# Three gemm groups of a decoder layer turned round, and the first modulation vector summed in two halves, with late constants loaded from another queue

## The chip, the cores and the metric

The program runs on one core of one Trainium2 chip. The metric is the device time of one execution in microseconds, the median of several runs. One further execution was recorded by the hardware profiler; its own time is 1817.8 us and its span, from the first to the last instruction, is 1816.1 us.

## What is computed

One layer of a decoder on 256 tokens of width 2048 in float32, cut here to what the change touches (S = 256, D = 2048):

```python
mod = silu(c) @ w_ada + b_ada                        # six vectors of 2048: sh1, sc1, gt1, sh2, sc2, gt2
h = rmsnorm(x, g_mix) * (1 + sc1) + sh1
z = h @ w_in                                         # mq mk mv mo mi mf dq dk dv sq sk sv gm gd gs
mqk = silu(causal_dwconv(concat(mq, mk), w_mconv))   # width 4, along the tokens
out_m, out_d, out_s = mlstm(...), differential_attention(...), stick_breaking_attention(...)
merged = (sigmoid(gm) * (out_m @ w_branch[0])
          + sigmoid(gd) * (out_d @ w_branch[1])
          + sigmoid(gs) * (out_s @ w_branch[2]))
x = x + gt1 * (merged @ w_out)
h = rmsnorm(x, g_ffn) * (1 + sc2) + sh2
x = x + gt2 * ((silu(causal_dwconv(h @ w_up[:, :DFF])) * (h @ w_up[:, DFF:])) @ w_down)
```

## The kernel before

Every large product keeps float32 accuracy with a rounded type: each operand is split into a high part (type fp32r, written by ScalarE) and a low part (the rest, written by VectorE as source minus high), and a product is three matmuls: high by high, high weight by low activation, low weight by high activation. `weights` (L310) loads a block of up to 512 rows by 512 columns through the SyncE queue into `raw`, and makes `hi` (L324, ScalarE) and `lo` (L326, VectorE) of it, two k-tiles of 128 rows at a time. `gemm` (L332) walks the contraction in steps of four k-tiles and has three forms for a chunk of 512 output columns:

- form F: a 128x128 block of weights is stationary and 256 tokens of one part of the activation move; the output has features on partitions. With 16 k-tiles that is 16 x 4 x 3 = 192 matmuls of 256 columns (L371).
- form T: 128 tokens of the activation are stationary and 512 weight columns move; the output has tokens on partitions. 16 x 2 x 3 = 96 matmuls of 512 columns (L369).
- form H: weights are stationary and both parts of the activation lie side by side, so that a high weight block takes them in one matmul of 512 columns and a low one takes the high part alone (256 columns): 64 + 64 matmuls (L355). Only the second half of the layer (the `w_up` product) uses it. Its output bank holds two halves, which ScalarE (L970) and VectorE (L971) add together.

Order of the work: x is loaded and normalised; `ada_first(0)` multiplies the first 256 columns of `sh1` and `sc1` out of `w_ada`: VectorE multiplies each k-tile of the weight by its scalar of silu(c) and adds it to one accumulator tile, 16 steps one after another (`ada_mac`, L206), and TensorE then sums that accumulator over the partitions with four small matmuls (`ada_sums`, L224; each shows as two instructions in the trace). From that `make_h` (L422) forms k-tiles 0 and 1 of h. Then the first thirteen chunks of `w_in` (sq, sk, sv and the block of gates and d-vectors) are worked through in stages of k-tiles 0 to 1, 2 to 3, 4 to 7, 8 to 11 and the rest (`partial`, L484), while VectorE goes on with the remaining columns of sh1 and sc1. `late_vectors` (L137) loads fourteen small constant vectors on the SyncE queue into a tile of slot 3, which x holds until it is transposed, and puts them on partitions.

Next come, each chunk with its weights: the four gate chunks of gs (`gates`, L797), the branch of stick-breaking attention (`branch`, L803, which multiplies the branch product by its gate), mo and mv in form T, mq and mk in form F with the convolution read straight from PSUM (L868 to L883), the branch of differential attention with its gates, the branch of the mLSTM with its gates, `w_out` in form T, and the feed-forward half. All gates and branch products are in form F. In the last branch (order 2) the finished merged sum, which has features on partitions already, is split into the two parts that `w_out` needs. `w_out` and `w_down` are in form T. Two queues of generators, `side` (the three mixers) and `ada` (the other modulation vectors), are pumped by `tick` at fixed rates between the steps of the gemms, so their VectorE, ScalarE and small TensorE work is traced between the large products; a compile-time scheduler then fixes each engine's order. `tc.issue_after` only fixes order on one engine; it adds no wait.

The two parts of h lie in two tiles `hh` and `hl`, each all sixteen k-tiles of one part.

Of the kernel before, what the change touches and what calls it, by code (L numbers as in the profile page):

```python
# [10 lines left out]
F32 = mybir.dt.float32  # L11
F32R = mybir.dt.float32r
# [5 lines left out]
P = 128  # L18
# [21 lines left out]
def kernel(  # L40
# [97 lines left out]
    def late_vectors():  # L138
        rows = slot(3, "rows2")
        rowsB, rowsC = rows[0:27, 0:P], rows[0:64, P:2 * P]  # L140
        rowsD = rows[0:NF, 2 * P:5 * P].rearrange("k (j p) -> k j p", j=3)
        ld = nc.sync.dma_start
        ld(rowsB[0:16], g_ffn[0].rearrange("(k p) -> k p", p=P))
        ld(rowsB[16:24], g_mout[0].rearrange("h (k p) -> (h k) p", p=P))
        ld(rowsB[24:25], g_dsub)
        for r in range(2):
            ld(rowsB[25:26, r * 64:(r + 1) * 64], g_dq)
            ld(rowsB[26:27, r * 64:(r + 1) * 64], g_dk)
        ld(rowsC, w_mconv[0].rearrange("j (k p) -> (j k) p", p=P))
        ld(rowsD, w_ffconv[0].rearrange("j (k p) -> k j p", p=P))  # L150
        ld(bif, b_gate_if.rearrange("o (g h) -> h (o g)", h=MH))
        lamv = rows[0:1, 640:896].rearrange("o (v d) -> o v d", v=4)
        for i, lv in enumerate((lam_q1, lam_k1, lam_q2, lam_k2)):
            ld(lamv[:, i, :], lv)
        yield
        pv = adaps.tile([P, 512], F32, tag="adaps", name="pv")
        T.transpose(pv[:, 0:27], rowsB, ident[:27, :27])
        T.transpose(pv[:, 27:91], rowsC, ident[:64, :64])
        for j in range(3):
            T.transpose(pv[:, 91 + NF * j:91 + NF * (j + 1)], rowsD[:, j, :], ident[:NF, :NF])  # L160
        A.copy(cols, pv[:, 0:223])
        yield
        V.tensor_scalar(gsub_c, gsub_c, 1.0 - LAM_INIT, None, ALU.mult)
        V.tensor_scalar(gdq_c, gdq_c, 64.0 ** -0.5, None, ALU.mult)

        lp = rows[0:1, 896:1024].rearrange("o (v d) -> o v d", v=2)
        V.tensor_tensor(lp, lamv[:, 0::2, :], lamv[:, 1::2, :], ALU.mult)
        ls = const.tile([1, 2], F32, name="ls")
        V.tensor_reduce(ls, lp, AX.X, ALU.add)
        A.activation(ls, ls, AF.Exp)  # L170
        nl = const.tile([1, 1], F32, name="nl")
        V.scalar_tensor_tensor(nl, ls[:, 1:2], -LAM_INIT, ls[:, 0:1], ALU.add, ALU.subtract)
        yield
        plam = adaps.tile([P, 512], F32, tag="adaps", name="plam")
        T.matmul(plam[:, 0:1], lhsT=ones[0:1, :], rhs=nl, start=True, stop=True)
        V.tensor_copy(nlam, plam[:, 0:1])
# [28 lines left out]
    def ada_mac(accs, raw, kt0, nk):  # L205
        for k in range(nk):  # L206
            kt = kt0 + k
            acc = accs[kt % len(accs)]
            if kt < len(accs):
                V.tensor_scalar(acc, raw[:, k, :], ccol[:, kt:kt + 1], None, ALU.mult)  # L210
            else:
                V.scalar_tensor_tensor(acc, raw[:, k, :], ccol[:, kt:kt + 1], acc, ALU.mult, ALU.add)  # L212

    def partition_sums(acc):

# [20 lines left out]
    def ada_first(k0):  # L236

        accs = [adap.tile([P, 512], F32, tag="acc", name="acc", bufs=2)]
        for q in range(4):
            raw = rawp.tile([P, 4, 512], F32, tag="raw", name="raw")  # L240
            step = 2 if k0 == 0 and q == 3 else 4
            for j in range(0, 4, step):
                for i in range(2):
                    r0, c0 = q * 512 + j * P, i * D + k0 * P
                    with tc.issue_after(state["load"].ins) if k0 else nullcontext():
                        load = nc.sync.dma_start(raw[:, j:j + step, i * 256:(i + 1) * 256],
                                                 w_ada[r0:r0 + step * P, c0:c0 + 256].rearrange("(k p) f -> p k f", p=P))
            if k0 == 0:
                state["load"] = load
            with tc.issue_after(state["first"].ins) if k0 == 2 and q == 0 else nullcontext():  # L250
                ada_mac(accs, raw, 4 * q, 4)
            yield
        ada_sums(accs, k0, 2)
# [131 lines left out]
    def split(hi, lo, src):  # L385

        A.copy(hi, src)
        return V.tensor_tensor(lo, src, hi.bitcast(F32), ALU.subtract)


    hh = slots.tile([P, KD, S], F32R, tag="hh", name="hh")
    hl = slots.tile([P, KD, S], F32R, tag="hl", name="hl")
    hact = (lambda kt: hh[:, kt, :], lambda kt: hl[:, kt, :])
    xnT = [slot(8, "xnT0"), slot(9, "xnT1")]
    xnT_k = lambda kt: xnT[kt // 8][:, (kt % 8) * S:(kt % 8 + 1) * S]

# [25 lines left out]
    def make_h(kt0, kt1):  # L422
        ts = []
        for kt in range(kt0, kt1):
            t = small("ht")
            ts.append(t)
            if kt0 == 0:
                A.activation(hh[:, kt, :], xnT_k(kt), AF.Identity, scale=a1[:, kt:kt + 1], bias=b1[:, kt:kt + 1])
                V.tensor_scalar(t, xnT_k(kt), a1[:, kt:kt + 1], b1[:, kt:kt + 1], ALU.mult, ALU.add)
                state["split"] = V.tensor_tensor(hl[:, kt, :], t, hh[:, kt, :].bitcast(F32), ALU.subtract)  # L430
            else:
                A.activation(t, xnT_k(kt), AF.Identity, scale=a1[:, kt:kt + 1], bias=b1[:, kt:kt + 1])
                state["split"] = split(hh[:, kt, :], hl[:, kt, :], t)
        if kt0 == 0:
            state["first"] = state["split"]
        state["h"] = kt1
# [3 lines left out]
    next(h0)  # L440
    norm_x(xt)
    for _ in h0:
        pass


    sqT, skT, sv = slot(0, "sqT"), slot(1, "skT"), slot(2, "sv")[:, 0:2048]
# [37 lines left out]
    def partial(ci, kt0, kt1):  # L484
        orient, col0, n, dest, scale = first[ci]
        while state["h"] < kt1:
            pump(ada, 1)
        pin = kt0 == 0 and ci == 1
        if kt0 == 0 and ci < 2:
            kept[ci] = [bank("kept"), bank("kept")]  # L490
        acc = gemm(orient, hact, w_in, 0, col0, n, kt0, kt1, hold=state["first"] if pin else None, hold_all=pin,
                   acc=kept.get(ci))
        for b in range(2):
            for cs, d in dest(b):
                if ci in kept:
                    if kt1 == KD:
                        A.activation(d, shaped(acc[b][:, cs], d), AF.Copy, scale=scale)
                elif kt0 == 0:
                    A.activation(d, shaped(acc[b][:, cs], d), AF.Copy, scale=scale)  # L499
                else:  # L500
                    V.scalar_tensor_tensor(d, shaped(acc[b][:, cs], d), scale, d, ALU.mult, ALU.add)  # L501
        tick()
# [288 lines left out]

    mg = []

    def mg_of(ch, b):
        return mg[ch // 2][:, (ch % 2) * 1024 + b * 512:(ch % 2) * 1024 + (b + 1) * 512]

    def gates(col_g, ch, dst):  # L797
        acc = gemm("F", hact, w_in, 0, col_g + ch * 512, 512, 0, KD)
        for b in range(2):
            A.activation(dst(ch, b), acc[b], AF.Sigmoid)  # L800
        tick()

    def branch(bi, col_g, act, order):  # L803
        for ch in range(4):
            if order == 0:
                sg = [mg_of(ch, 0), mg_of(ch, 1)]
            else:
                sg = [wide("sg"), wide("sg")]
                gates(col_g, ch, lambda c_, b: sg[b])
            accb = gemm("F", act, w_branch[bi], 0, ch * 512, 512, 0, KM)  # L810
            for b in range(2):
                d = mg_of(ch, b)
                V.tensor_tensor(sg[b], accb[b], sg[b], ALU.mult)
                if order:
                    V.tensor_tensor(d, d, sg[b], ALU.add)
                if order == 2:
                    h0 = (ch % 2) * 4 + 2 * b
                    split(mgh[ch // 2][:, h0:h0 + 2, :], mgl[ch // 2][:, h0:h0 + 2, :],
                          d.rearrange("p (a t) -> p a t", a=2))
            tick()  # L820


# [14 lines left out]
    rates["ada"] = 0.9  # L837
    mg.append(slot(8, "mg0"))
    for ch in range(2):
        gates(C_GS, ch, mg_of)  # L840
    drain(side)
    mg.append(slot(9, "mg1"))
    side.append(diff())
    rates["side"] = 2.6
    for ch in range(2, 4):
        gates(C_GS, ch, mg_of)
    branch(2, C_GS, stick.out, 0)
    drain(side)

# [16 lines left out]
    rates["ada"] = 0.2  # L866
    for t, col0, f0 in ((mqT, C_MQ, 0), (mkT, C_MK, 8)):
        for ch in range(2):  # L868
            acc = gemm("F", hact, w_in, 0, col0 + ch * 512, 512, 0, KD)
            y = t[:, ch * 1024:(ch + 1) * 1024]  # L870
            for f in range(4):
                src = acc[f // 2][:, (f % 2) * S:(f % 2 + 1) * S]
                yf = y[:, f * S:(f + 1) * S]
                wc = lambda j: mconv_c[:, j * 16 + f0 + ch * 4 + f:j * 16 + f0 + ch * 4 + f + 1]
                A.activation(yf, src, AF.Copy, scale=wc(3))
# [160 lines left out]
```

## Time and profile before

| | |
|---|---|
| median of 3 runs | 1816.47 us (1816.28 to 1816.69) |
| the profiled execution | 1817.8 us, span 1816.1 us |
| TensorE busy | 1774.3 us, 98% of the span |
| VectorE busy | 1333.4 us, 73% |
| ScalarE busy | 907.1 us, 50% |
| GpSimd busy | 9.5 us, 1% |
| read from memory | 419.68 MB, 232 GB/s over the span |
| mean granted TensorE clock | 0.994 |

PE is TensorE's matmul stream, PEld its weight loads, DVE is VectorE, ACT is ScalarE, POOL is GpSimd, SP is SyncE (it only issues DMAs here). A line such as L371 is a line of the kernel before. In a stream of matmuls the end of each is modelled, so one matmul's duration says less than the time from the start of one to the start of the next: that is read from a long unbroken piece in the chain of work that ended last, as its length over its count.

### The profile page before, as it was taken

What the parts mean: (1) busy time and instruction counts of PE and PEld (TensorE: products, weight loads), DVE (VectorE), ACT (ScalarE), POOL (GpSimd) and SP (SyncE); (2) the same over time, 40 slices, a digit from 0 to 9 for tenths busy, and PEclk for the clock granted to TensorE, in tenths of its full rate; (3) what the DMA queues carried; (4) which work ended last, traced back from release to release, by engine and by line L of the source; (5) the groups of instructions that cost most, each with busy time, mean ns of one, the idle gap of its engine ahead of it and who ended that gap; (6) DMA issues with size and microseconds to landing.
All of it is one profiled execution on the core that took longest, in us unless ns stands there. A gap on an engine that the chain in (4) does not pass through costs nothing.

```text
span 1816.1 us, 27533 instructions
## 1 busy us (share of the span) xinstructions
PE 1774.3 (98%) x11045; PEld 1605.4 (88%) x11045; DVE 1333.4 (73%) x1787; ACT 907.1 (50%) x1221; POOL 9.5 (1%) x30
## 2 busy tenths in 40 slices
PE   4989999999999999999999999999999999999998
PEld 4888999999988999999999878888888888888887
DVE  5998867887888687686897568888875556666654
ACT  5533345666565554543444465555553335555532
POOL 0000000000000000000000000000000000000000
PEclk9989999999999999999999999999999999999999
DMA  9988965766778467677898547777765555555563
GB/s 300 338 299 295 315 199 165 262 233 212 240 251 276 163 218 257 219 239 268 286 316 279 184 152 248 254 263 273 263 207 191 197 192 186 188 189 192 196 209 116
DMA packets 219644, 423.55 MB, mean 233 GB/s; under 512 B 8768, under 2 KB 31613, under 8 KB 219005
## 3 DMA queue, kind: packets, MB, share of 16 engines
q1 hardware_dynamic: 217693, 417.56, 68.5%
q0 software_dynamic: 544, 2.11, 0.3%
q8 instruction: 86, 1.41, 0.3%
q10 hardware_dynamic: 1280, 2.14, 0.3%
q14 instruction: 41, 0.34, 0.1%
HBM read 419.68 MB, written 2.10 MB: 232 GB/s over the span
## 4 chain that ended last, share of the span: by engine, by line
PE 91%; DVE 3%; DMA 3%; ACT 1%; issue 1%; SPq 0%; DVEq 0%; ACTq 0%
PE gp L369 30%; PE gp L371 29%; PE acch L355 27%; PE kept L371 2%; DMA raw<-in_w_in_dram 2%; DMA raw<-in_w_ada_dram 1%; DVE lo L326 1%; DVE quads L212 1%; PE psc L627 0%; ACT hi L324 0%; PE pm L228 0%; PE pr L303 0%; DVE acc L212 0%; PE px L935 0%; PE ptf L685 0%
## 5 line engine op out<-in xcount | busy, mean ns | idle before, releaser
L326 DVE TENSOR_TENSOR lo<-raw,hi 128x1024 fp32r<-128x1024 f32 (+1 forms) x608 | 728.1, 1207 | 364.4 <-ACT hi L324 338.1
L324 ACT CAST hi<-raw 128x1024 fp32r<-128x1024 f32 (+1 forms) x608 | 622.7, 1038 | 706.5 <-PE gp L369 225.5
L355 PE MATMUL acch<-h,hi 128*128 128x512 f32 x1408 | 427.9, 395 | 1.8 <-DVE h L952 1.8
L371 PE MATMUL gp<-hh,hi 128*128 128x256 f32 x1152 | 299.8, 285 | 2.3 <-ACT skT L499 2.2
L355 PEld LDWEIGHTS acch<-h,lo 128*128 128x128 f32 x1408 | 252.5, 188 | 54.1
L371 PE MATMUL gp<-hl,hi 128*128 128x256 f32 x1152 | 298.3, 283 | 0.0
L355 PE MATMUL acch<-h,lo 128*128 128x256 f32 x1408 | 263.7, 279 | 0.0
L355 PEld LDWEIGHTS acch<-h,hi 128*128 128x128 f32 x1408 | 221.6, 189 | 10.6 <-DVE h L952 2.0
L371 PEld LDWEIGHTS gp<-hh,hi 128*128 128x128 f32 x1152 | 220.9, 192 | 4.0 <-ACT skT L499 2.4
L371 PEld LDWEIGHTS gp<-hl,hi 128*128 128x128 f32 x1152 | 220.9, 192 | 0.2
L371 PE MATMUL gp<-hh,lo 128*128 128x256 f32 x1152 | 218.3, 284 | 0.5 <-DVE lo L326 0.5
L212 DVE SCALAR_TENSOR_TENSOR acc<-araw,ccol,acc 128x512 f32<-128x512 f32 x240 | 178.8, 745 | 4.0 <-DMA araw<-in_w_ada_dram 2.1
L371 PEld LDWEIGHTS gp<-hh,lo 128*128 128x128 f32 x1152 | 173.2, 192 | 1.1 <-DVE lo L326 0.7
L369 PE MATMUL gp<-hi,hh 128*128 128x440 f32 (+1 forms) x416 | 159.9, 384 | 3.6 <-DVE sv L501 1.4
L369 PE MATMUL gp<-hi,hl 128*128 128x440 f32 (+1 forms) x416 | 158.1, 380 | 0.0
L369 PE MATMUL gp<-hi,ath 128*128 128x512 f32 x352 | 137.0, 389 | 0.0
L369 PE MATMUL gp<-hi,atl 128*128 128x512 f32 x352 | 136.9, 389 | 0.0
L369 PE MATMUL gp<-lo,hh 128*128 128x440 f32 (+1 forms) x416 | 112.9, 378 | 2.3 <-DVE lo L326 2.3
L369 PE MATMUL gp<-lo,ath 128*128 128x512 f32 x352 | 105.8, 389 | 0.0
L369 PEld LDWEIGHTS gp<-hi,hh 128*128 128x128 f32 x416 | 79.3, 191 | 15.8 <-PE gp L369 2.4
L369 PEld LDWEIGHTS gp<-lo,hh 128*128 128x128 f32 x416 | 78.0, 189 | 13.7 <-DVE lo L326 3.6
L369 PEld LDWEIGHTS gp<-hi,hl 128*128 128x128 f32 x416 | 79.3, 191 | 10.4 <-issue 0.7
(346 smaller groups left out, 2059.9 us busy)
## 6 DMA issues: line engine op xcount, KB each, us to landing
raw<-in_w_in_dram SPq DMA_DIRECT2D x98, 1024.0 KB, 5.0
raw<-in_w_up_dram SPq DMA_DIRECT2D x88, 1024.0 KB, 5.1
araw<-in_w_ada_dram SPq DMA_DIRECT2D x128, 512.0 KB, 5.4
raw<-in_w_down_dram SPq DMA_DIRECT2D x44, 1024.0 KB, 5.1
raw<-in_w_ada_dram SPq DMA_DIRECT2D x62, 512.0 KB, 5.2
raw<-in_w_branch_dram SPq DMA_DIRECT2D x24, 1024.0 KB, 5.3
raw<-in_w_in_dram SPq DMA_DIRECT2D x21, 880.0 KB, 4.7
raw<-in_w_out_dram SPq DMA_DIRECT2D x16, 1024.0 KB, 5.2
```

The source lines that it names most:

```text
L212: V.scalar_tensor_tensor(acc, raw[:, k, :], ccol[:, kt:kt + 1], acc, ALU.mult, ALU.add)
L324: A.copy(hi[:, :, :n], raw[:, k0:k0 + 2, :n])
L326: state["split"] = V.tensor_tensor(lo[:, :, :n], raw[:, k0:k0 + 2, :n], hi[:, :, :n].bitcast(F32), ALU.subtract)
L355: T.matmul(acc[t][:, 0:m], lhsT=w[k // 2][:, k % 2, sl], rhs=ah(s0 + k)[:, 0:m], start=start, stop=s0 + k == kt1 - 1 and w is wl, skip_gro ...
L369: T.matmul(o, lhsT=a(s0 + k)[:, sl], rhs=wk[:, :n], **kw)
L371: T.matmul(o, lhsT=wk[:, sl], rhs=a(s0 + k), **kw)
```

## The change

Six things at once. (1) `late_vectors` issues its fourteen loads from GpSimd's queue in place of SyncE's. (2) `ada_first(0)` sums even and odd k-tiles into two accumulators (both then go through `ada_sums`), and the `lo` of the first `w_in` chunk is ordered behind the last of these steps on VectorE. (3) h is kept as k-tiles with both parts side by side, in two tiles of eight k-tiles. (4) gates and branch products are in form T; the merged sum then has tokens on partitions, so in the last branch it is transposed by TensorE, 128x128 at a time, before it is split. (5) mq and mk are in form H; the two halves are added into a tile `msum`, from which the convolution reads. (6) The pump rate of `side` in one stretch goes from 2.6 to 2.9.

```diff
-        ld = nc.sync.dma_start
+        def ld(*args):
+            with tc.issue_after(state["load"].ins):
+                nc.gpsimd.dma_start(*args)
...
         accs = [adap.tile([P, 512], F32, tag="acc", name="acc", bufs=2)]
+        if k0 == 0:
+            accs.append(sidewide("acc2"))
...
-    hh = slots.tile([P, KD, S], F32R, tag="hh", name="hh")
-    hl = slots.tile([P, KD, S], F32R, tag="hl", name="hl")
-    hact = (lambda kt: hh[:, kt, :], lambda kt: hl[:, kt, :])
+    h1 = [slots.tile([P, KD // 2, 2 * S], F32R, tag=t, name="h1") for t in ("hh", "hl")]
+    h1act = lambda kt: h1[kt // 8][:, kt % 8, :]
+    hact = (lambda kt: h1act(kt)[:, 0:S], lambda kt: h1act(kt)[:, S:2 * S])
...
     for _ in h0:
-        pass
+        state["mac0"] = state["mac"]
...
-        pin = kt0 == 0 and ci == 1
+        if kt0 == 0 and ci == 0:
+            state["first"], done = state["mac0"], state["first"]
+        pin = kt0 == 0 and ci < 2
...
     def gates(col_g, ch, dst):
-        acc = gemm("F", hact, w_in, 0, col_g + ch * 512, 512, 0, KD)
-        for b in range(2):
-            A.activation(dst(ch, b), acc[b], AF.Sigmoid)
+        acc = gemm("T", hact, w_in, 0, col_g + ch * 512, 512, 0, KD)
+        for tt in range(NT):
+            A.activation(dst[tt], acc[tt], AF.Sigmoid)
         tick()
...
-            accb = gemm("F", act, w_branch[bi], 0, ch * 512, 512, 0, KM)
-            for b in range(2):
-                d = mg_of(ch, b)
-                V.tensor_tensor(sg[b], accb[b], sg[b], ALU.mult)
+            accb = gemm("T", act, w_branch[bi], 0, ch * 512, 512, 0, KM)
+            for tt in range(NT):
+                d = mg_of(ch)[tt]
+                V.tensor_tensor(sg[tt], accb[tt], sg[tt], ALU.mult)
                 if order:
-                    V.tensor_tensor(d, d, sg[b], ALU.add)
-                if order == 2:
-                    h0 = (ch % 2) * 4 + 2 * b
+                    V.tensor_tensor(d, d, sg[tt], ALU.add)
+            if order == 2:
+                for k2 in range(2):
+                    pb = bank("pmg")
+                    for tt in range(NT):
+                        for j in range(2):
+                            k = 2 * k2 + j
+                            T.transpose(pb[:, j * S + tt * P:j * S + (tt + 1) * P], mg_of(ch)[tt][:, k * P:(k + 1) * P],
+                                        ident)
+                    h0 = (ch % 2) * 4 + 2 * k2
                     split(mgh[ch // 2][:, h0:h0 + 2, :], mgl[ch // 2][:, h0:h0 + 2, :],
-                          d.rearrange("p (a t) -> p a t", a=2))
+                          pb.rearrange("p (a t) -> p a t", a=2))
...
-    rates["side"] = 2.6
+    rates["side"] = 2.9
...
-            acc = gemm("F", hact, w_in, 0, col0 + ch * 512, 512, 0, KD)
+            acc = gemm("H", h1act, w_in, 0, col0 + ch * 512, 512, 0, KD)
             y = t[:, ch * 1024:(ch + 1) * 1024]
+            sums = [sidewide("msum"), sidewide("msum")]
             for f in range(4):
-                src = acc[f // 2][:, (f % 2) * S:(f % 2 + 1) * S]
+                src = sums[f // 2][:, (f % 2) * S:(f % 2 + 1) * S]
+                A.copy(src, acc[f][:, S:2 * S])
+                V.tensor_tensor(src, acc[f][:, 0:S], src, ALU.add)
```

## Rows read from the trace of the kernel before

**Rows 1.** The page's busy times, share of the span and counts.
```profile
PE 1774.3 (98%) x11045; PEld 1605.4 (88%) x11045; DVE 1333.4 (73%) x1787; ACT 907.1 (50%) x1221; POOL 9.5 (1%) x30
```

**Rows 2.** Windows by stage: PE, PEld, DVE, ACT, POOL busy; clock, DMA share, GB/s.
```profile
0.00:230.00 230.00, 197.37 (x1173) 181.24 (x1174) 191.02 (x253) 106.44 (x149) 2.42 (x16) 0.96 0.91 309
...
410.00:500.00 90.00, 90.00 (x736) 85.94 (x736) 73.16 (x131) 54.94 (x112) 0.00 (x0) 1.00 0.67 224
...
645.00:785.00 140.00, 140.00 (x1123) 136.60 (x1122) 106.82 (x172) 73.19 (x107) 0.00 (x0) 1.00 0.65 225
785.00:983.00 198.00, 198.00 (x1651) 197.61 (x1650) 157.88 (x191) 85.81 (x96) 2.52 (x5) 1.00 0.82 279
```

**Rows 3.** The chain that ended last: start, length, what, matmuls in it.
```profile
559.38 1.31 PE ptf L685 x12
560.69 33.60 PE gp L369 x148
...
785.63 51.84 PE gp L371 x432
...
1185.34 55.84 PE acch L355 x320
```

**Rows 4.** Windows of the start, columns as in rows 2.
```profile
25.00:30.00 5.00, 2.54 (x11) 2.45 (x12) 2.90 (x9) 2.78 (x4) 0.00 (x0) 0.58 0.56 172
...
40.00:70.00 30.00, 27.30 (x147) 24.53 (x145) 27.00 (x35) 23.00 (x45) 0.00 (x0) 1.00 1.04 364
70.00:125.00 55.00, 48.10 (x275) 43.08 (x276) 52.92 (x72) 19.53 (x26) 0.00 (x0) 0.91 0.88 312
```

**Rows 5.** VectorE's timeline: start, time from first start to last end.
```profile
15.54 8.63 DVE L212 SCALAR_TENSOR_TENSOR acc<-raw,ccol,acc 128x512 f32<-128x512 f32 x11 [0.18 <-DMA raw<-in_w_ada_dram]
24.32 1.22 DVE L326 TENSOR_TENSOR lo<-raw,hi 128x1024 fp32r<-128x1024 f32 x1 [0.15 <-ACT hi L324]
...
54.51 0.74 DVE L212 SCALAR_TENSOR_TENSOR acc<-raw,ccol,acc 128x512 f32<-128x512 f32 x1
55.17 1.28 DVE L212 SCALAR_TENSOR_TENSOR quads<-raw,ccol,quads 128x1024 f32<-128x1024 f32 x1
```

**Rows 6.** The chain at the start: TensorE's sum over partitions.
```profile
26.26 1.88 PE pm L228 x8
```

**Rows 7.** SyncE's queue at the start: start, time until issued, load.
```profile
17.34 1.49 SPq L319 DMA_DIRECT2D raw<-in_w_in_dram  x3
...
20.69 1.85 SPq L143 DMA_DIRECT2D rows<-in_g_ffn_dram  x1
...
23.25 0.24 SPq L147 DMA_DIRECT2D rows<-in_g_dq_dram  x1
24.59 0.22 SPq L148 DMA_DIRECT2D rows<-in_g_dk_dram  x1
...
28.94 0.39 SPq L319 DMA_DIRECT2D raw<-in_w_in_dram  x1
```

**Rows 8.** ScalarE's timeline at the start: the first two casts of w_in.
```profile
23.24 1.04 ACT L324 CAST hi<-raw 128x1024 fp32r<-128x1024 f32 x1 [1.73 <-DMA raw<-in_w_in_dram]
24.60 1.04 ACT L324 CAST hi<-raw 128x1024 fp32r<-128x1024 f32 x1 [0.31 <-DMA raw<-in_w_in_dram]
```

**Rows 9.** Waits from 20 to 125 us: total us, times, longest.
```profile
PE gp L371 <- ACT skT L499: 2.2, 1, 2.2
```

**Rows 10.** GpSimd's issue, its load's landing, and VectorE's first use of late vectors.
```profile
897.59 0.49 POOL L297 DMA_DIRECT2D br<-in_b_ada_dram  x1 [32.15 <-DVE acc L212]
...
br<-in_b_ada_dram POOLq DMA_DIRECT2D x8, 2.0 KB, 4.2
...
36.78 0.28 DVE L167 TENSOR_TENSOR rows<-rows 1x128 f32<-1x128 f32 x1 [0.56 <-DMA rows<-in_lam_k_dram]
```

**Rows 11.** Form H's two evacuation lines: ns min/median/max, first and last start.
```profile
L970 ACT COPY gsum<-acch x44: 352/372/373, 1097.0 to 1681.8; 128x256 f32<-128x256 f32 x44
...
L971 DVE TENSOR_TENSOR gsum<-acch,gsum x44: 411/418/425, 1097.6 to 1683.3; 128x256 f32<-128x256 f32 x44
```

More of the change, by code (lines that the diff above doesn't have):

```diff
@@ L426, in make_h @@
             ts.append(t)
+            hi, lo = hact[0](kt), hact[1](kt)
             if kt0 == 0:
-                A.activation(hh[:, kt, :], xnT_k(kt), AF.Identity, scale=a1[:, kt:kt + 1], bias=b1[:, kt:kt + 1])
+                A.activation(hi, xnT_k(kt), AF.Identity, scale=a1[:, kt:kt + 1], bias=b1[:, kt:kt + 1])
                 V.tensor_scalar(t, xnT_k(kt), a1[:, kt:kt + 1], b1[:, kt:kt + 1], ALU.mult, ALU.add)
-                state["split"] = V.tensor_tensor(hl[:, kt, :], t, hh[:, kt, :].bitcast(F32), ALU.subtract)
+                state["split"] = V.tensor_tensor(lo, t, hi.bitcast(F32), ALU.subtract)
             else:
                 A.activation(t, xnT_k(kt), AF.Identity, scale=a1[:, kt:kt + 1], bias=b1[:, kt:kt + 1])
-                state["split"] = split(hh[:, kt, :], hl[:, kt, :], t)
+                state["split"] = split(hi, lo, t)
         if kt0 == 0:
@@ L492, in partial @@
                    acc=kept.get(ci))
+        if kt0 == 0 and ci == 0:
+            state["first"] = done
         for b in range(2):
@@ L792, with mg_of @@
     mg = []
-    def mg_of(ch, b):
-        return mg[ch // 2][:, (ch % 2) * 1024 + b * 512:(ch % 2) * 1024 + (b + 1) * 512]
     def gates(col_g, ch, dst):
-        acc = gemm("F", hact, w_in, 0, col_g + ch * 512, 512, 0, KD)
-        for b in range(2):
-            A.activation(dst(ch, b), acc[b], AF.Sigmoid)
+        acc = gemm("T", hact, w_in, 0, col_g + ch * 512, 512, 0, KD)
+        for tt in range(NT):
+            A.activation(dst[tt], acc[tt], AF.Sigmoid)
         tick()
+    def mg_of(ch):
+        o = (ch % 2) * 512
+        return [mg[ch // 2][:, tt * 1024 + o:tt * 1024 + o + 512] for tt in range(NT)]
     def branch(bi, col_g, act, order):
@@ L805, in branch @@
             if order == 0:
-                sg = [mg_of(ch, 0), mg_of(ch, 1)]
+                sg = mg_of(ch)
             else:
                 sg = [wide("sg"), wide("sg")]
-                gates(col_g, ch, lambda c_, b: sg[b])
-            accb = gemm("F", act, w_branch[bi], 0, ch * 512, 512, 0, KM)
-            for b in range(2):
-                d = mg_of(ch, b)
-                V.tensor_tensor(sg[b], accb[b], sg[b], ALU.mult)
-                if order:
-                    V.tensor_tensor(d, d, sg[b], ALU.add)
-                if order == 2:
-                    h0 = (ch % 2) * 4 + 2 * b
+                gates(col_g, ch, sg)
+            accb = gemm("T", act, w_branch[bi], 0, ch * 512, 512, 0, KM)
+            for tt in range(NT):
+                d = mg_of(ch)[tt]
+                V.tensor_tensor(sg[tt], accb[tt], sg[tt], ALU.mult)
+                if order:
+                    V.tensor_tensor(d, d, sg[tt], ALU.add)
[8 more added lines that the diff above has]
+                    h0 = (ch % 2) * 4 + 2 * k2
                     split(mgh[ch // 2][:, h0:h0 + 2, :], mgl[ch // 2][:, h0:h0 + 2, :],
-                          d.rearrange("p (a t) -> p a t", a=2))
+                          pb.rearrange("p (a t) -> p a t", a=2))
             tick()
@@ L839 @@
     for ch in range(2):
-        gates(C_GS, ch, mg_of)
+        gates(C_GS, ch, mg_of(ch))
     drain(side)
@@ L843 @@
     side.append(diff())
-    rates["side"] = 2.6
+    rates["side"] = 2.9
     for ch in range(2, 4):
-        gates(C_GS, ch, mg_of)
+        gates(C_GS, ch, mg_of(ch))
     branch(2, C_GS, stick.out, 0)
```

2 lines of the change are left out of this document (1 added, 1 removed).

## Prediction

> **What bounds the kernel now.** I read the busy times first: TensorE is busy for 1774.3 of 1816.1 us [rows 1]. Busy alone proves little, since an engine can be busy with matmuls that wait, so I split it by stage [rows 2]. Up to 230 us TensorE works for 197.4 us, which leaves 32.6 us of idleness; the whole span has 1816.1 - 1774.3 = 41.8, so only 9.2 us of idleness lie behind 230 us. The chain of work that ended last says the same from the other end: behind the start it is nearly all long unbroken pieces of matmuls. So two questions decide. In the long part: how many TensorE microseconds does the change remove from the stream? At the start: which idleness goes?
>
> The stream's price per matmul comes from unbroken pieces [rows 3]: form F 51.84 / 432 = 0.120 us for 256 columns, form T 33.60 / 148 = 0.227 us for 512 columns, form H 55.84 / 320 = 0.1745 us as the mean of its 512 and 256. A 512-column matmul is thus cheaper by 0.013 us than two of 256.
>
> **Gates and branches in form T.** A gate chunk goes from 192 x 0.120 = 23.04 us to 96 x 0.227 = 21.79 us: 1.25 us less. There are 12 (four of gs, four each of gd and gm): 14.9 us. A branch chunk has half the k-tiles, 11.52 against 10.90: 0.62 us less, 12 of them: 7.5 us. All of it lies in TensorE's stream, which is busy without a break in these stages [rows 2], and the row for form T comes from mo and mv, which use the same h in the same form, so both bounds are these two prices. The evacuations keep their number and size (two of 128x512 per chunk on the same engines), so I cost them at nothing.
>
> The Trainium skill, page TensorE: Matmul & The Clock Gate, section Back-to-back issue gap, gives for the spacing of matmuls alone N/2.4 + 2.5 ns, so an estimate by that page is 109 ns for 256 columns and 216 ns for 512; by it a gate chunk would fall only from 20.97 to 20.72 us, and all gates and branches together would bring 4.4 us. This case's rows show 120 and 227 ns, about 11 ns more for either length, and that fixed part is what halving the number of matmuls saves; the measurement decides.
>
> **The transposes.** Form T leaves the merged sum with tokens on partitions, so the last branch adds 4 chunks x 2 banks x 4 = 32 transposes at 1.31 / 12 = 0.109 us [rows 3]: 3.5 us in the stream. Each group waits for two VectorE multiplications and additions; TensorE meanwhile has the next chunk's gates, and after the last chunk the first three quarters of `w_out`'s contraction. If that cover were gone, a group would cost some 3 us, 12 us for four.
>
> **mq and mk in form H.** A chunk goes from 23.04 to 128 x 0.1745 = 22.34 us: 0.70 us less, four chunks, 2.8 us. Added: 16 ScalarE copies of 0.372 us and 16 VectorE additions of 0.418 us [rows 11], 6.0 and 6.7 us; VectorE is busy for 106.8 of 140 us in the stage that holds most of it [rows 2], so they lie beside the matmuls. If there were no room, they would cost 6.7 us. The form takes two banks from the pool of the side work, which has none to do until mk is finished.
>
> Long part: 14.9 + 7.5 + 2.8 - 3.5 = 21.7 us. With TensorE some 5% quicker, VectorE's share rises from about 80% to 85% in the two branch stages [rows 2], so I allow 0.5 us for new short waits (bounds 0 and 4).
>
> **Two accumulators.** Steps on one accumulator follow each other at (8.63 - 0.75) / 10 = 0.79 us, while a step behind one on another tile starts after 55.17 - 54.51 = 0.66 us [rows 5]. The data of the second quarter was there at 15.54. Twelve steps from there at 0.66 end at 23.5 us, in place of 26.2 us, where the `lo` of 1.22 us had come in between the last two [rows 5, 6]. Against that, the sum over partitions is 16 instructions of 1.88 / 8 = 0.235 us [rows 6]; the first eight can begin with the even accumulator finished at 22.9, so all end at about 26.6 us in place of 28.1. Gain 1.5 us. Below: if steps stayed at 0.79, the doubled sum would eat what moving the `lo` gives, gain 0. Above: 2.7 us, if the first eight sums were fully hidden.
>
> The Trainium skill, page VectorE: DVE Perf Modes, section The DRAIN you can't avoid, says that the next VectorE instruction does not start until the pipe is empty and that no chaining avoids this (it adds that one that is not held starts earlier); taken strictly, alternating tiles gives nothing, which is the lower bound above. The two spacings of this trace, 0.79 and 0.66 us, disagree with the strict reading.
>
> **Loads on GpSimd's queue.** On SyncE, the small loads begin at 20.69 us, and the two at 23.25 and 24.59 are held until the moments at which ScalarE starts on newly landed weights [rows 7, 8]: the queue waits there for earlier transfers to finish. The fourth `w_in` load is behind them, at 28.94. Its buffer is free once the first `lo` is done, about 25.5 us, so it could go out 3.4 us earlier, and the next ones, also behind small loads, more. Between 25 and 30 us the DMA engines move 172 GB/s against 364 from 40 to 70 [rows 4]: 5 x (1 - 172/364) = 2.6 us of transfer time are lost there. TensorE later stands for 2.2 us because ScalarE, waiting for such weights, evacuates late [rows 9]. What is to be had beyond the first 1.5 us lies between 0 (the transfers from 40 us on run at full rate, so earlier issue only queues) and 4.8 us (2.6 + 2.2). I take 1.8, nearer to the single wait of rows 9, because VectorE is next in line: from 70 to 125 us it is busy for 52.9 of 55 us and TensorE for 48.1 [rows 4]. GpSimd pays 14 issues of about 0.49 us, nothing else being queued there [rows 10].
>
> Rate 2.9, the new layout of h and the same-size splits have no cost of their own.
>
> **Sum.** 21.7 - 0.5 + 1.5 + 1.8 = 24.5 us. Against the profiled execution (1817.8 us, 1.7 around its span) that is 1793.3; the median of the runs is 1816.5, so I forecast 1792.0.
>
> **Rivals.** (a) *The start gives nothing.* VectorE's full stretch from 70 to 125 us takes back any lead, or the new order there costs a little: gain 18 to 21.5, 1795 to 1798.5. For: rows 4. Against: VectorE has idle time at 25 to 30 and 40 to 70, so its work can move up.
> (b) *The side work sets the pace.* If VectorE can't be packed tighter where the mixers run, the stages 410 to 500 and 645 to 785 keep their length. By their counts [rows 2] the first holds the four branch chunks of gs (384 of 736 matmuls) and at most 352 / 192 = 1.8 gate chunks, 2.5 + 2.3 us; the second two mk chunks (384 of 1123) and at most 739 / 288 = 2.6 pairs of gate and branch, 1.4 + 4.8. So up to 11 us are lost: gain 13.5, 1803. For: VectorE at 81% and 76%, in chains with ScalarE. Against: TensorE has no idleness there today, so they are not the bound yet; the pump rate rises too.
> (c) *The turn does nothing*: a 512-column matmul in these stages costs two of 256, as would follow if only columns counted. Then 2.8 - 3.5 + 3.3 = 2.6 us are left, 1814; under the estimate by that page's figures it would be about 1810, and I carry both as one. Against: form T at 0.227 us on the same h.
> (d) *Slower: GpSimd's loads hold up VectorE.* VectorE's order is fixed; at 36.78 us it multiplies the four lam vectors [rows 10], and all `lo` work stands behind. A load from GpSimd takes 4.2 us to land [rows 10]. Fourteen one after another from 20.7 us would be there at 79.5, and VectorE would stand for up to 43 us: 24.5 - 43 = 18.5 us slower, 1835. It decides against the change once the last lam load lands later than 24.5 us behind VectorE's place for it, about 61 us. Against: they are independent, and two overlapping rounds land by about 40 us; the scheduler also knows them as loads and can place the product later.
>
> **Chances.** Forecast (gain 21.5 to 31, 1785.5 to 1795) 0.67; (a) 0.18; (b) 0.08; (c) 0.03, about half of it too near to tell; (d) 0.03; better than 1785.5 0.01. About 0.2%, 3.6 us, is what a measurement of this kernel can tell from no change. The range takes forecast and (a) and the bounds of the waits allowed for, 1785.5 to 1801. Faster by over 0.2%: forecast, (a), (b), half of (c), 0.95; within 0.2% 0.02; slower 0.03.
>
> **What would show it.** Right: 512-column matmuls at 0.227 us in the gate and branch stages, the last stage of rows 2 (1651 / 288 = 5.7 pairs) shorter by 5.7 x 1.87 - 3.5 = 7 us, form H at 0.1745 in mq and mk; the sum over partitions ending near 26.6 us, the fourth `w_in` load issued near 25.5 us, TensorE idle for under 30 us in the first 230. Wrong: waits of TensorE on VectorE's `lo` or on transposes in the branches, VectorE waiting for a late vector, or TensorE idle for more than 12 us behind 230 us.

## The result, and the profile after

The changed kernel takes 1801.37 us (median of 4 runs, 1797.52 to 1802.34) against 1816.38 us (median of 4 beside it): a ratio of 0.9912, 95% interval 0.9899 to 0.9926, 15.0 us less. The forecast was 1792.0 us, 24.5 us less, with a range up to 1801.0. So the sign was right, the size fell 9.5 us short, and the median lies 0.4 us above the range. The profiled execution is 1802.06 us, its span 1800.1 us: 16.0 us less than before.

The page's busy times and the windows of the stages after (columns as in [rows 2]; the last window runs from and to the same instructions as that group's last row):

```profile
PE 1761.4 (98%) x9101; PEld 1507.7 (84%) x9101; DVE 1336.3 (74%) x1803; ACT 913.4 (51%) x1237; POOL 16.5 (1%) x44
```

```profile
0.00:225.00 225.00, 198.04 (x1181) 182.29 (x1182) 190.36 (x253) 106.61 (x149) 9.92 (x30) 0.96 0.92 316
...
566.00:572.00 6.00, 2.94 (x20) 2.04 (x18) 5.96 (x11) 2.06 (x6) 0.12 (x1) 1.00 0.77 262
...
772.09:963.80 191.71, 191.71 (x858) 158.06 (x857) 156.24 (x189) 85.97 (x96) 2.52 (x5) 1.00 0.84 288
```

Three readings. The start has 27.0 us without TensorE in place of 32.6 [rows 2]: the same instructions come 5.2 us earlier from about 230 us on. The last stage has gone from 198.0 to 191.7 us: 6.3 us, or 5.6 with the last eight of the 32 transposes, which stand behind the window, where 7 were forecast. And there is a hole where before there was none: 3.1 us idle between 566 and 572. It brings the idleness behind the start to 11.7 us, from 9.2; the prediction had set 12 as its sign of being wrong, so idle time alone does not show what is missing.

The prices per matmul are the forecast ones. Pieces of the chain of work that ended last, after (start, length, what, matmuls in it):

```profile
22.84 3.54 PE pm L231 x16
...
403.79 24.08 PE gp L374 x106
...
589.10 50.95 PE acch L360 x292
...
904.08 24.92 PE gp L374 x109
```

Form T costs 24.08 / 106 = 0.2272 us in a gate stage and 24.92 / 109 = 0.2286 us in the last branch, form H 50.95 / 292 = 0.1745 us: forecast 0.227 and 0.1745.

What is new is where the mixers' small steps stand. Stick-breaking's `po` products and the last transposes of the differential mixer, `ptf`, with the normalisation of `od` ahead of them; in the kernel before (duration ns min/median/max, first and last start):

```profile
L580 PE MATMUL po<-ez,sv x16: 377/379/382, 317.8 to 395.4; 128*128 128x256 f32 x16
```

```profile
L675 DVE TENSOR_TENSOR od<-od,ro x2: 1217/1218/1219, 552.5 to 553.7; 128x1024 f32<-128x1024 f32 x2
```

The same views of the kernel after:

```profile
L590 PE MATMUL po<-ez,sv x16: 377/379/382, 312.6 to 403.2; 128*128 128x256 f32 x16
```

```profile
L685 DVE TENSOR_TENSOR od<-od,ro x2: 1218/1218/1218, 566.9 to 568.1; 128x1024 f32<-128x1024 f32 x2
```

The first `po` is 5.2 us earlier than before, the last 7.8 us later, and `od` 14.4 us later, although the large products around them run ahead. TensorE's timeline shows what that costs:

```profile
566.17 0.61 PE L374 MATMUL gp<-lo,h 128*128 128x512 f32 x2
568.31 0.63 PE L695 MATMUL ptf<-ident,od 128*128 128x128 f32 x4 [1.52 <-DVE od L685]
569.35 1.53 PE L695 MATMUL ptf<-ident,od 128*128 128x128 f32 x12 [0.42 <-DVE od L685]
572.04 1.19 PE L374 MATMUL gp<-hi,h 128*128 128x512 f32 x4 [1.16 <-ACT mv L881]
```

It waits for `od`, and then for ScalarE to empty a bank into mv, whose slot is `od`'s: mv can't be written until the last `ptf` has read `od`. In the kernel before, `ptf` went straight into the next product [rows 3].

### The profile page after: what moved, and what is told of

Read it like the earlier page. It is cut to its first block, busy times and chain, and to the rows that moved or that the text cites. A ratio compares the mean times of both kernels' runs of the same rounds, so it can differ in the third digit from the quotient of the medians.

```text
span 1800.1 us, 23693 instructions
## 1 busy us (share of the span) xinstructions
PE 1761.4 (98%) x9101; PEld 1507.7 (84%) x9101; DVE 1336.3 (74%) x1803; ACT 913.4 (51%) x1237; POOL 16.5 (1%) x44
## 4 chain that ended last, share of the span: by engine, by line
PE 91%; DVE 5%; DMA 2%; issue 1%; ACT 1%; SPq 0%; ACTq 0%; DVEq 0%
PE gp L374 51%; PE acch L360 32%; PE kept L376 2%; PE gp L376 2%; DVE quads L215 1%; DVE lo L331 1%; DMA raw<-in_w_in_dram 1%; DMA raw<-in_w_ada_dram 1%; PE psc L637 1%; ACT hi L329 0%; SPq L251 0%; PE pm L231 0%; DVE dv L511 0%; DVE acc L215 0%; PE px L956 0%
## 5 line engine op out<-in xcount | busy, mean ns | idle before, releaser
L360 PE MATMUL acch<-h,hi 128*128 128x512 f32 x1664 | 504.5, 396 | 1.8 <-DVE h L973 1.8
L374 PE MATMUL gp<-hi,h 128*128 128x512 f32 (+1 forms) x1600 | 409.0, 385 | 5.2 <-DVE dq L511 1.2
L374 PEld LDWEIGHTS gp<-hi,h 128*128 128x128 f32 x1600 | 296.6, 188 | 56.9 <-issue 4.4
L374 PE MATMUL gp<-lo,h 128*128 128x512 f32 (+1 forms) x800 | 228.4, 384 | 0.6 <-DVE lo L331 0.6
L374 PEld LDWEIGHTS gp<-lo,h 128*128 128x128 f32 x800 | 149.6, 188 | 27.4 <-DVE lo L331 1.5
L374 PEld LDWEIGHTS gp<-lo,ath 128*128 128x128 f32 x352 | 66.1, 188 | 13.7
L374 PEld LDWEIGHTS gp<-hi,ath 128*128 128x128 f32 x352 | 66.1, 188 | 13.7
L374 PEld LDWEIGHTS gp<-hi,atl 128*128 128x128 f32 x352 | 66.1, 188 | 13.6
L215 DVE SCALAR_TENSOR_TENSOR quads<-raw,ccol,quads 128x1024 f32<-128x1024 f32 x45 | 57.5, 1279 | 2.9 <-DMA raw<-in_w_ada_dram 2.7
L374 PE MATMUL gp<-hi,mgl 128*128 128x512 f32 x128 | 50.3, 393 | 0.0
## 6 DMA issues: line engine op xcount, KB each, us to landing
araw<-in_w_ada_dram SPq DMA_DIRECT2D x128, 512.0 KB, 5.6
raw<-in_w_ada_dram SPq DMA_DIRECT2D x62, 512.0 KB, 5.9
```

The costliest lines, as they stand in the source:

```text
L215: state["mac"] = V.scalar_tensor_tensor(acc, raw[:, k, :], ccol[:, kt:kt + 1], acc, ALU.mult, ALU.add)
L360: T.matmul(acc[t][:, 0:m], lhsT=w[k // 2][:, k % 2, sl], rhs=ah(s0 + k)[:, 0:m], start=start, stop=s0 + k == kt1 - 1 and w is wl, skip_gro ...
L374: T.matmul(o, lhsT=a(s0 + k)[:, sl], rhs=wk[:, :n], **kw)
```

## The experiments

Every kernel was timed beside the kernel before on the same chip; times are medians, ratios against the kernel before with 95% intervals.

**The change in its three parts.** The start alone (accumulators, loads, the `lo` held behind the sums):

```diff
+        if k0 == 0:
+            accs.append(sidewide("acc2"))
...
+                nc.gpsimd.dma_start(*args)
```

> The kernel before with the start alone changed (loads on GpSimd's queue, two accumulators, the first lo behind them). In the changed kernel the last of the early chunks is evacuated 5.2 us sooner than before, and nothing behind 230 us can take that back if the parts are independent: about 1811 us, 5 us less. Rival: the lead is lost again in the chains of the mixers, 1814 to 1816 us.

Measured: 1812.79 us against 1816.14, ratio 0.9980 (0.9971 to 0.9988): 3.35 us less, between the two expectations. Forecast for this part: 3.3.

Gates and branches in form T, with the transposes:

```diff
-        acc = gemm("F", hact, w_in, 0, col_g + ch * 512, 512, 0, KD)
+        acc = gemm("T", hact, w_in, 0, col_g + ch * 512, 512, 0, KD)
```

> The kernel before with gates and branches in form T alone, pump rate kept at 2.6. Theory: the matmuls bring about 18 us and the transposes take 3, but the chains of the mixers fall behind and TensorE waits for them near the mv product, some 6 us: about 1807 us. Rival: the waits come from the other parts, and form T alone keeps its gain: about 1801 us. Recorded forecast for these parts: 1816.5 - 14.9 - 7.5 + 3.5 = 1797.6 us.

Measured: 1808.52 us, ratio 0.9958 (0.9945 to 0.9971): 7.6 us less. Forecast 14.9 + 7.5 - 3.5 = 18.9. The missing part is here.

mq and mk in form H, with the layout of h that it needs:

```diff
-            acc = gemm("F", hact, w_in, 0, col0 + ch * 512, 512, 0, KD)
+            acc = gemm("H", h1act, w_in, 0, col0 + ch * 512, 512, 0, KD)
```

> The kernel before with mq and mk in form H alone. By the matmul prices 2.3 to 2.8 us less: about 1814 us, whatever the other parts do. Rival: the added copies and additions are late and take it back: 1816 us or more.

Measured: 1813.16 us, ratio 0.9982 (0.9973 to 0.9991): 3.0 us less. Forecast 2.8. The three sum to 14.0, the whole change gives 15.0: they add up, and only form T falls short, by some 11 us. Not all of that is in its stages: in the run's profile the stretch from the last `kept` matmul (261.0 us) to the first `prb` one (1061.9) is 10.8 us shorter than before's, 8.1 less than forecast, and behind it, ahead of the feed-forward half, the granted clock averaged 0.67 from 1061 to 1065 us and 0.50 from 1065 to 1069, where it stayed at 1.00 in the profile of before.

**mv behind mq and mk**, in the kernel after, to give the differential mixer's end more time:

```diff
-    mv = slots.tile([P, NT, MH, MDH + 1], F32, tag="s2", name="mv")
...
     mqT, mkT = slot(3, "mqT"), slot(4, "mkT")
...
+    mv = slots.tile([P, NT, MH, MDH + 1], F32, tag="s2", name="mv")
```

> The changed kernel with the mv product placed behind mq and mk in the program, so that it no longer needs, right after mo, the slot that differential attention still holds. Theory (TensorE waits there for the late chain of differential attention): 4 to 7 us less than the changed kernel, about 1796 us. Rival (form T simply costs more per matmul among other work, no late chain): no change, about 1801 us.

Measured: 1809.16 us, ratio 0.9962 (0.9949 to 0.9976): about 8 us slower than after, against both expectations. TensorE's waits between 540 and 560 us of this kernel (total us, times, longest):

```profile
PE ptf L695 <- DVE od L685: 6.7, 1, 6.7
PE pa L662 <- DVE dsc L658: 1.4, 1, 1.4
```

The wait for `od` has grown from 1.9 to 6.7 us: in this order no large product stood ahead of `ptf`. Behind it the granted clock averaged 0.53 from 554 to 560 us, so part of the 8 us is the clock's. That form H needs two of the mixers' banks, and so couldn't go ahead, is how I read it; it wasn't tried by itself. The run does show that the end of this mixer is what TensorE waits for.

**Without the mixers**, before and after:

```diff
-            side.append(stick())
+            stick.out = hact
...
-    side.append(diff())
+    diff.out = hact
...
-    side.append(mlstm(mqT, mkT, sig))
+    mlstm.out = hact
```

> Edit: the kernel before with the three mixers (the stick, the difference and the normaliser mixer between gates and branches) left out: each branch multiplies its gate and its product with the hidden activation itself, so this run's time lacks the mixers' whole work; it serves only as the pair of the next run. No theory speaks of its absolute time beyond: the mixers' small matmuls and transposes in the stretch from 233 to 1083 us go, so well over 100 us less than 1816. What is tested is the difference to the next run.

> Edit: the kernel after with the same three mixers left out. Theory (the part of the forecast gain that is missing is in the mixers: their steps come later in TensorE's order, by 25 us of stream at the fourth stick group and 18 us at the last difference step, so that their tails are covered by less stream and TensorE waits there): with no mixers nothing is left to wait for, and this run is 21 to 25 us below the run with the mixers left out of the kernel before, near the forecast 24.5. Rival (the 512-column matmuls in place of two 256-column ones save less by themselves than the trace's durations say, about 9 us less over gates and branches): the difference stays at 13 to 17 us, as with the mixers.

Measured: 1761.60 us (1758.83 to 1762.54) with the kernel before, 1738.12 us (1737.38 to 1740.75) with the kernel after: the difference is 23.5 us, inside the theory's 21 to 25, and against 15.0 with the mixers. In the kernel after without mixers the trace names two waits of TensorE behind 225 us, the two ahead of the feed-forward half that the kernel before has as well:

```profile
PE prb L950 <- DVE dg L947: 2.0, 1, 2.0
PE acch L360 <- DVE h L973: 1.8, 1, 1.8
```

So the terms of the sum are nearly all there, and 8.5 us of them are lost where the mixers run. Medians of four runs leave this uncertain by some 2 us. The traces give it without the start and without the clock ahead of the feed-forward half: the last `kept` matmul stands behind the first 230 us, the first `prb` one at the end of `w_out`, and the clock is at 1.00 all the way between them (each line gives the durations, then the first and the last start). Without the mixers, before and after:

```profile
L371 PE MATMUL kept<-hh,lo x128: 278/283/415, 32.5 to 259.9; 128*128 128x256 f32 x128
L929 PE MATMUL prb<-dg,ones x4: 275/384/583, 1017.4 to 1019.1; 128*128 128x128 f32 x4
```

```profile
L376 PE MATMUL kept<-h,lo x128: 278/283/387, 30.4 to 258.7; 128*128 128x256 f32 x128
L950 PE MATMUL prb<-dg,ones x4: 275/312/377, 994.3 to 995.8; 128*128 128x128 f32 x4
```

With the mixers, before and after:

```profile
L371 PE MATMUL kept<-hh,lo x128: 278/283/415, 33.2 to 263.2; 128*128 128x256 f32 x128
L929 PE MATMUL prb<-dg,ones x4: 275/312/377, 1074.9 to 1076.4; 128*128 128x128 f32 x4
```

```profile
L376 PE MATMUL kept<-h,lo x128: 278/283/415, 30.5 to 258.0; 128*128 128x256 f32 x128
L950 PE MATMUL prb<-dg,ones x4: 275/382/417, 1056.7 to 1058.7; 128*128 128x128 f32 x4
```

Without the mixers the stretch goes from 757.5 to 735.6 us, 21.9 less, where the matmuls and transposes were forecast at 21.7; with them from 811.7 to 798.7, 13.0 less. So 8.9 us are lost there.

**mv out of `od`'s slot**, in the kernel after (x's tile and one other in slot 3 are cut to 2048 as well):

```diff
-        n = NT * MH * (MDH + 1) + 8 if i == 2 else 2048
+        n = NT * MH * (MDH + 1) + 8 if i in (2, 3) else 2048
...
-    mv = slots.tile([P, NT, MH, MDH + 1], F32, tag="s2", name="mv")
+    mv = slots.tile([P, NT, MH, MDH + 1], F32, tag="s3", name="mv")
...
-    mqT, mkT = slot(3, "mqT"), slot(4, "mkT")
+    mqT, mkT = slot(2, "mqT")[:, 0:2048], slot(4, "mkT")
```

> Edit: the kernel after, but the mv product is written into slot 3 (made 16 elements per partition wider) and mqT into slot 2, in place of the other way round, so that mv no longer shares a slot with the difference's output od and mqT takes it 16 products later. The last transposes of the difference then stand behind 16 us of stream, as in the kernel before, in place of 7. Theory (TensorE's three waits between 566 and 572 us, 3.6 us in all, come from this): 2.5 to 4 us less than after, 1797.5 to 1799. Rival (those waits only move: the difference's transposes are needed by the end of the branch, and VectorE is late there too): within 1 us of after.

Measured: 1796.45 us (1795.56 to 1799.60), ratio 0.9897 (0.9882 to 0.9912): 4.9 us less than after's median (by the two ratios 2.7, and their intervals overlap). TensorE's three waits between 566 and 572 us are gone from the trace. That looked like the proof; the next run shows that it is not. And from the last `kept` matmul (252.9 us) to the first `prb` one (1050.5) it is only 1.1 us shorter than after's: summed from start to start, form T's matmuls take back some 3.5 us, at 229 ns in place of 227.

**The same swap in the kernel before**, as a control:

> Edit: the kernel before with mv in slot 3 and mqT in slot 2, the same swap as in the run on the kernel after, and nothing else. It tells whether the 4 to 5 us that the swap brought there belong to the change. Theory (they do: in the kernel before 15 us of stream cover the end of the difference mixer, and its trace shows no wait of TensorE there that the swap could remove): within 1.5 us of before, 1815 to 1818. Rival (the swap is a gain of its own, which the kernel before lacked as much as the kernel after): 3 to 5 us below before, 1812 to 1814.

Measured: 1796.54 us (1795.33 to 1797.99) against 1815.42, ratio 0.9898 (0.9882 to 0.9915): **18.9 us less, more than the whole change gives, and both expectations are wrong.** Every engine but GpSimd has the same instructions in the same order as in the kernel before, and on GpSimd only one memset of mv has moved. Pieces of the chain, the same ones in either kernel, first before:

```profile
251.94 11.51 PE kept L371 x96
263.45 11.52 PE gp L371 x96
```

and with the swap:

```profile
247.84 10.90 PE kept L371 x96
258.74 10.88 PE gp L371 x96
...
559.82 25.64 PE gp L369 x112
...
927.54 33.16 PE gp L371 x288
```

The same 96 matmuls of 256 columns of form F take 10.88 in place of 11.52 us: 0.1133 us each, not 0.120. In the last stage they take 33.16 / 288 = 0.115. Form T takes 25.64 / 112 = 0.229, not 0.227. Two matmuls of 256 columns now cost 0.227 to 0.230 and one of 512 costs 0.229: **the saving on which the change rests is not there**, and indeed with the swap the kernel after (0.9897 of before) is no faster than the kernel before (0.9898); from the last `kept` matmul (258.5 us here) to the first `prb` one (1053.9) it is even some 2 us longer. The gain begins 300 us ahead of mv, so the exchange of slots can't be its cause.

What differs from the first instruction on is memory: slot 3 is 16 elements, 64 bytes per partition, wider, and all tiles allocated behind it lie 64 bytes further on. The weights' `hi` and `lo` are among them, the two parts of h are not. The change itself moves neither: in the kernel after they lie as in the kernel before. In the kernel before, the program's own layout puts the first `hi` block 147456 bytes, 36 times 4096, behind `hh`. The other pairs of a moving tile and a weight tile bear this out in part, as the median time from the start of one matmul to the next: where both moved, odh (slot 6) by hi, 120 ns stays 120; where only the weights moved, osh (slot 3) by hi goes from 120 to 118 and hh by hi from 120 to 114. But osl (slot 4), whose matmuls alternate with osh's, moved with the weights and goes from 120 to 118 too, and omh (slot 1), which also moved with them, had 117 before and has 119 with the swap. So that the place of the tiles sets the price is shown, and which distance does it is not. No run moved the tiles by 64 bytes and left the slots as they were, nor by another distance, and why the place matters stays open.

The Trainium skill, page SBUF — State Buffer, section Who interferes with whom, gives TensorE two independent read ports, one for the moving operand and one for the weights, and says that it never waits on anyone. Taken strictly, that leaves no room for the place of a tile to matter. These runs show 0.120 against 0.1133 us, with the granted clock at 1.00 in both windows, and the measurement decides; that the two reads meet is not shown either.

**The start's two terms.**

```diff
-        ld = nc.sync.dma_start
+        def ld(*args):
+            with tc.issue_after(state["load"].ins):
+                nc.gpsimd.dma_start(*args)
```

> Edit: the kernel before, and of the change only the start's loads put on GpSimd's queue (weights as they were, one accumulator). The prediction's terms: 1.8 of the 3.3 at the start come from these loads, 1.5 from the two accumulators; together they measured 3.35 us. If the two terms stand as written, this run is 1.8 us below before, 1814.3. Rival (the loads pay only where the sums also end earlier, or the accumulators do all): 0 to 0.5 us below, with the other 3 us from the accumulators.

Measured: 1814.51 us against 1816.67, ratio 0.9989 (0.9979 to 0.9999): 2.2 us less. And the accumulators alone, with their `lo` held behind:

```diff
+        if k0 == 0:
+            accs.append(sidewide("acc2"))
```

> Edit: the kernel before, and of the change only the two accumulators of the first adaLN vector (with the low parts held behind the sums). The prediction gave this 1.5 us of the 3.3 at the start; the loads alone measured 2.2 us (with an interval from 0.2 to 3.8), both together 3.35. If the two add up as the prediction has it: 1.2 to 1.5 us below before. Rival (the sums set nothing, since TensorE's next wait takes over what they end earlier): 0 to 0.4 us.

Measured: 1814.71 us against 1817.18, ratio 0.9989 (0.9980 to 0.9998): 2.5 us less. The terms 1.8 and 1.5 lie within either interval, and so would 2.0 and 2.5; the two sum to 4.6 by themselves and gave 3.35 together. The split isn't settled better than that.

**The pump rate back to 2.6**, in the kernel after:

```diff
-    rates["side"] = 2.9
+    rates["side"] = 2.6
```

> Edit: the kernel after with the mixers' pump rate in the gates at 2.6, as the kernel before had it, in place of 2.9. Theory (the rate does not set where the mixers' steps stand: with it at 2.6 in the run with the gates and branches alone, they stood at the same places of TensorE's stream as in the kernel after): within 1 us of after. Rival (the rate of 2.9 brings the mixers' steps forward, and the change would lose more without it): 2 us or more above after.

Measured: 1798.99 us (1798.16 to 1803.11), ratio 0.9906 (0.9890 to 0.9921). The median is 2.4 us below after's, which neither expected; the ratios differ by 0.0006, well inside the intervals, and the last `po` stands at 402.9 us against 403.2. The rate does nothing that can be measured. Single executions differ by such an amount through the clock alone: in this run's profile it averaged 0.60 from 572 to 578 us, behind the waits for `od`, and stayed at 1.00 ahead of the feed-forward half, and in after's profile it was the other way round.

**Work in TensorE's two idles ahead of the feed-forward half**, on top of the swap in the kernel after:

```diff
+        if ch == 3:
+            fb = bank("fill")
+            for _ in range(14):
+                T.matmul(fb[:, 0:S], lhsT=mgh[0][:, 0, 0:P], rhs=mgh[1][:, 7, :], start=True, stop=True)
...
+    for _ in range(13):
+        with tc.issue_after(lastt.ins):
+            T.matmul(fb[:, 0:S], lhsT=mgh[0][:, 0, 0:P], rhs=mgh[1][:, 7, :], start=True, stop=True)
```

> Edit: the run with mv in slot 3, and 14 matmuls of 256 columns more ahead of the first prb matmul of the last w_out chunk and 13 behind the second, into a bank that nobody reads: 1.7 and 1.6 us of work in TensorE's two idles of 2.2 and 2.1 us ahead of the FFN. Theory (in some executions the granted clock falls to 0.5 behind these idles, which costs about 2 us and makes the spread of the runs): the granted clock stays at 1.00 there, and the median falls by 1 to 3 us against the run with mv in slot 3, whose median was 1796.45. Rival (the idles are longer than the trace shows or the extra matmuls stand in the way of the two products that VectorE waits for): the same or 1 to 3 us more.

Measured: 1794.02 us (1792.54 to 1796.66), ratio 0.9876 (0.9861 to 0.9890), the fastest of all; 2.4 us below the run without the fillers, as the theory had it, though the two intervals overlap. The windows of the two idles (columns as in [rows 2]), in the kernel before, the kernel after, the swap without fillers, and with them:

```profile
1070.00:1074.00 4.00, 2.91 (x13) 2.06 (x11) 2.50 (x5) 2.81 (x5) 0.00 (x0) 1.00 0.79 264
1074.00:1078.00 4.00, 1.79 (x12) 1.42 (x12) 2.60 (x8) 3.12 (x9) 0.00 (x0) 1.00 0.00 0
```

```profile
1052.00:1056.00 4.00, 2.70 (x12) 1.89 (x11) 2.72 (x5) 2.81 (x5) 0.00 (x0) 1.00 0.78 262
1056.00:1060.00 4.00, 2.47 (x12) 2.20 (x12) 1.92 (x8) 2.77 (x8) 0.00 (x0) 0.64 0.01 2
1060.00:1064.00 4.00, 2.99 (x8) 2.53 (x9) 4.00 (x9) 3.16 (x8) 0.00 (x0) 0.50 0.00 0
```

```profile
1050.00:1054.00 4.00, 2.72 (x12) 2.46 (x12) 1.68 (x6) 2.71 (x8) 0.00 (x0) 0.58 0.00 0
1054.00:1058.00 4.00, 2.98 (x8) 2.50 (x9) 4.00 (x9) 3.17 (x8) 0.00 (x0) 0.50 0.01 2
```

```profile
1050.00:1054.00 4.00, 3.65 (x30) 3.27 (x29) 2.56 (x9) 3.12 (x9) 0.00 (x0) 1.00 0.20 76
1054.00:1058.00 4.00, 3.69 (x25) 3.18 (x24) 4.00 (x9) 3.12 (x9) 0.00 (x0) 1.00 0.00 0
```

TensorE had the same instructions and the same two idles in before and in after; in the profile of before the clock stayed at 1.00, in that of after it fell behind the first idle, to a mean of 0.64 in the second window and to 0.50, the lower level of 1.2 GHz, in the third. The swap without fillers shows the fall too. With the fillers the clock stays up, and all four timed runs show a mean clock of 0.996, where the five without them range from 0.993 to 0.995.

## Why the prediction was right or wrong

**Prices per matmul: right in this layout, for a reason that fell.** 0.227, 0.120 and 0.1745 us were read from the right pieces, and form T and form H cost that after the change too. But the step "that fixed part is what halving the number of matmuls saves" took 0.120 us for a property of a 256-column matmul. It hangs on where h and the weights lie: with the weights 64 bytes further on, the same matmuls cost 0.1133 us. So that halving the matmuls paid at all is luck of the layout, which no line of the prediction shows. The estimate by the Trainium skill's page TensorE: Matmul & The Clock Gate, section Back-to-back issue gap, 109 ns, was set aside because of a row that another layout does not repeat; 0.1133 us is still above it, and for 512 columns 0.227 and 0.229 stay above its 216 in either layout. Rival (c), "a 512-column matmul costs two of 256", which had a chance of 0.03, is false for the kernel as it was and true for it with the tiles moved.

**The allowance for new waits: this is the step that failed in size.** "I allow 0.5 us for new short waits (bounds 0 and 4)" was worked out from VectorE's share of busy time. Without the mixers the change is worth 23.5 us, near the sum of 24.5; with them 15.0. So the mixers cost 8.5 us by the medians and 8.9 by the traces, twice the upper bound. In the two profiles, TensorE's time from start to start, summed by kind from the first `po` to the last `prb`, splits the long part: form F's 512.0 us became 400.5 of form T and 89.4 of form H, a gain of 22.1 where 25.2 were forecast; everything else grew by 9.5 us, of which the transposes are 2.8 (forecast 3.5). Of the 8.9 us, the three waits at 566 to 572 us, 3.6 by this count, can be pointed at; some 4 are spread over the mixers' other small matmuls (0.2 to 1.9 us more in each group), the rest over form T's matmuls among them, and no run shows why these take longer. The low clock ahead of the feed-forward half, about 2 us in the profile of after, is not the mixers' doing: it shows without them too, in the profile of before without mixers. Rival (b) named the place, the mixers' stages, and its time, 1803, came nearest, but not its mechanism: VectorE did not fill up, at 156.2 of 191.7 us in the last stage. Behind the three waits stands one chain of small steps, which ended late because the compiled order puts them later. Why it puts them later is open; the pump rate is not the reason.

**Form H and the transposes: right.** 3.0 us for a forecast 2.8, and 2.8 us for a forecast 3.5; mq and mk take the 89.4 us that four chunks at 22.34 make. The copies and additions stayed beside the matmuls.

**The start: right in sum.** 3.35 us by runs for a forecast 3.3. The marks came where they were expected: VectorE's sums, SyncE's fourth `w_in` load and the lam product in the kernel after:

```profile
18.06 5.39 DVE L215 SCALAR_TENSOR_TENSOR acc<-raw,ccol,acc 128x512 f32<-128x512 f32 x8 [0.27 <-DMA raw<-in_w_ada_dram]
23.40 1.22 DVE L331 TENSOR_TENSOR lo<-raw,hi 128x1024 fp32r<-128x1024 f32 x1
...
41.98 0.27 DVE L170 TENSOR_TENSOR rows<-rows 1x128 f32<-1x128 f32 x1
```

```profile
24.65 0.37 SPq L324 DMA_DIRECT2D raw<-in_w_in_dram  x1
```

The steps end at 23.45 us (forecast 23.5), the sixteen sums at 22.84 + 3.54 = 26.4 (forecast 26.6), the load goes out at 24.65 (forecast 25.5). The eight steps are (5.39 - 0.74) / 7 = 0.66 us apart. The Trainium skill's page VectorE: DVE Perf Modes, section The DRAIN you can't avoid, read strictly, leaves alternating accumulators nothing; this spacing speaks against that reading here. The 2.5 us of their own run agree, though that run held the `lo` back as well. Rival (d) needed the lam product past 61 us; it runs at 41.98 with no wait ahead of it. Rival (a) fell with the start's 3.35 us.

**What is not settled.** Why the mixers' steps come later, and why their small matmuls take longer. How the place of a tile sets a matmul's price; whether 64 bytes alone do it. How much the vanished waits are worth by themselves: the swap also raised form T's price from 227 to 229 ns, which took back nearly all of them, and lowered what is left of form F from 120 to 113. The start's edits and the fillers on top of the swap in the kernel before, which by these runs might be the best of all, were not run.

## What to carry to other kernels

A price per instruction read from a long clean piece is a price of that layout too: before a form is changed for some 5% per matmul, move the tiles by a few bytes and read the price again. Here 64 bytes in one slot gave more than six edits. And the cost of side work is not its share of an engine: ask how much stream stands behind its last step and who needs its slot next, and put a control on the kernel before beside every experiment on the kernel after; without it the swap would have been told as proof.

## What the runs showed of the hardware that was not expected

The same 256-column matmuls at 0.120 or at 0.1133 us, with the granted clock at 1.00, by where the weights lie against the moving tile. The granted clock in the same two idles of some 2 us: at 1.00 through both in the profile of before, down to 0.50 behind the first of them in the profile of after, with the same instructions around them.
